# A new order for the first norm and for the last products of a hybrid RG-LRU / retention / conv-FFN block

## The chip, the cores and the metric

One core of one Trainium2 chip runs the whole program. The metric is device microseconds of one execution. Engines are named as the profile names them: PE is TensorE's matmul, PEld its weight load, DVE VectorE, ACT ScalarE, POOL GpSimd, SP SyncE.

## The reference, cut to what matters

The two ends of the computation are what the change touches: the norm of the 16 meta tokens and 512 input tokens ahead of the first projection, and the final product `w_down` with the last norm.

```python
def rms_norm(x, g):
    y = x32 * lax.rsqrt(jnp.mean(x32 * x32, axis=-1, keepdims=True) + EPS)
    return y * g
...
h = concatenate([meta_tokens, x])                 # 16 + 512 tokens, 1024 features, f32
xn = rms_norm(h, norm_mix_g)                      # first norm
z = xn @ w_in                                     # 8 parts: RNN, its gate, q, k, v, ...
... # convolution, RG-LRU, retention, mixing with w_out, h += ...
xn = rms_norm(h, norm_ffn_g)
up = causal_dwconv(xn @ w_up)
gate, val = split(up, 2)
h = h + (gelu(gate) * val) @ w_down               # 3072 -> 1024
out = rms_norm(h, norm_final_g)[:, 16:]           # final norm, meta tokens dropped
```

## The kernel before, in words

Products are f16 on TensorE. Each f32 operand is split by `split` into a high half (ScalarE, L91) and a low half (VectorE, L92), and a product is high*high + high*low + low*high. Weights come from HBM in units of at most 1 MB; SP issues their loads one after the other, ScalarE and VectorE split them into `wt` tiles, and TensorE uses them. In most of the program the tile scheduler places the instructions of each engine; within `manual_schedule` (at the start) PE, ACT and DVE keep the order in which the code is written. Each engine executes its own list in order.

At the start SP loads, in this order: 128 tokens of x, the norm's weights spread over 128 partitions (`gmix`, 512 KB), the meta tokens (16 partitions of 1024 features), the next 128 tokens, and then weights and the other tokens by turns. For one block of tokens `norm_rows` has ScalarE square and sum (L296) and take the root (L298), VectorE invert it (L300) and multiply by it and by `gmix` (L306, two halves); `norm_transpose` has TensorE transpose the rows (L313) into PSUM and `split` write them as `xh` and `xl`, the transposed f16 pair that all projections read. The blocks go 0, meta, 1, 2, 3. `keep_warm` (L392) fills TensorE with products of zeros meanwhile. `first_half(n)` (L359) is the left half (block 0, block 1 and the meta tokens) of the projection for 128 columns: 24 matmuls of 267 columns. After the last of the three first halves TensorE transposes small vectors (`ptv`) that POOL loaded by nine DMAs into `v1` and `v2`.

At the end the product with `w_down` is made as seven products by Strassen-like sums (`PRODUCTS`), for 256 columns of each half in each of two passes (`ps_`). In the last round of the second pass the seven products end one after the other, 12 matmuls each, and behind each VectorE adds what is complete (`add`, `total`), ScalarE sums squares (`square`), VectorE multiplies by the final norm's weights (`weigh`), `three_quarters` sums three of a token's four sums of squares, `inverse` takes the root with the fourth, and `rows_out` scales the rows, left half on VectorE and right half on ScalarE, and issues a 256 KB store for each. `h2p[1]` holds tokens 256 to 511 (`tt` 2 and 3), `h2p[0]` tokens 0 to 255.

Of the kernel before, what the change touches and what calls it, by code (L numbers as in the profile page):

```python
# [8 lines left out]
F32 = mybir.dt.float32  # L9
# [41 lines left out]
def hybrid_block_kernel(ctx, tc, x, meta, norm_mix_g, w_in, conv_w, conv_b, rg_a_w, rg_a_b,  # L51
# [235 lines left out]
    gmix_t = wsp.tile([P, D], F32, name="gmix", tag="wt")  # L287
    gmix = [gmix_t[:, a * 512:(a + 1) * 512] for a in range(2)]
# [33 lines left out]
    xmeta = wsp.tile([P, D], F32, name="xmeta", tag="wt")  # L322
# [47 lines left out]

    def first_rows(i):
        xn_t[i] = pair("xn")
        if i < 0:
            norm_rows(xmeta[:NM], NM, gmix, xn_t[i])
        else:
            norm_rows(xin[i // 2][:, i % 2], P, gmix, xn_t[i])

    def first_transpose(i):
        xn = xn_t.pop(i)
        if i < 0:  # L380
            norm_transpose(NM, xh[:, :, 3:3 + NM], xl[:, :, 3:3 + NM], S_XN, xn)
        else:
            c0 = 3 + NM + P * i
            norm_transpose(P, xh[:, :, c0:c0 + P], xl[:, :, c0:c0 + P], S_XN, xn)
# [25 lines left out]
    first_transpose(1)  # L410
# [4 lines left out]
    first_transpose(2)  # L415
# [5 lines left out]
    first_transpose(3)  # L421
# [678 lines left out]
    for j in range(12):  # L1100
# [10 lines left out]
        for m in range(2):  # L1111
# [3 lines left out]
            if f == KF - 1:  # L1115
# [11 lines left out]
    PRODUCTS = (("P1", "A11", "B11"), ("P6", "F6", "T2"), ("P7", "F7", "T3"), ("P4", "A22", "T4"),  # L1127
                ("P5", "F5", "T1"), ("P2", "A12", "B21"), ("P3", "F3", "B22"))
# [22 lines left out]
    def three_quarters(tt):  # L1151
        part0 = small.tile([P, 2], F32, name="part0")
        nc.vector.reduce_sum(part0[:, 0:1], sums[:, tt, 0:3], axis=mybir.AxisListType.X)
# [3 lines left out]
    def inverse(tt, part0):  # L1157
        sd = small.tile([P, 1], F32, name="sd")
        nc.scalar.activation(sd, sums[:, tt, 3:4], AF.Sqrt, scale=inv_d, bias=part0)
# [4 lines left out]
    def rows_out(tt, rs):  # L1164
        nc.vector.tensor_scalar_mul(h2[tt][:, 0:512], h2[tt][:, 0:512], rs)
        nc.sync.dma_start(o2[tt * P:(tt + 1) * P, 0:512], h2[tt][:, 0:512])
# [127 lines left out]
```

## Time and profile before

| | |
|---|---|
| median of 3 runs | 1090.39 us (1090.39 to 1091.27) |
| profiled execution | 1090.36 us, its span in the profile 1088.6 us |
| PE, PEld busy | 1064.8 us (98%), 867.7 us (80%) |
| DVE, ACT busy | 798.8 us (73%), 540.9 us (50%) |
| mean granted TensorE clock | 0.995 |
| moved by DMA | 112.01 MB, 103 GB/s over the span |

The span is from the first to the last instruction; the time of an execution has 1.8 us more around it. Starts in a timeline count from the span's start. A row of the timeline has start, length, engine, line, operation, what it writes and reads with shapes, how many instructions are merged in it, and in brackets the idle time of the engine before it with what ended it. The busy shares are means over stages with different limits: the first 28 us and the last 12 us are read by themselves below.

### The profile page before, as it was taken

The page shows a single profiled execution, that of the slowest core. Times are in us where ns is not written, and L with a number is a line of the kernel's source. Part 1 is how long each engine was busy: PE and PEld are TensorE (multiplying, and loading weights), DVE is VectorE, ACT ScalarE, POOL GpSimd, SP SyncE. Part 2 cuts the span into 40 slices and gives each one's busy share as a digit, 9 for nine tenths or more (in the row PEclk, how much of TensorE's full clock was granted, in tenths as well). Part 3 has the DMA queues.
Part 4 walks back from the last instruction along what each step waited for, and adds up shares of the span by engine and source line. Part 5 has one row for each costly group of instructions (what it writes and reads, how often), then busy time and mean ns, then how long its engine had stood idle before and what let it go on. Part 6 is the DMA issues. An engine that isn't in the chain of part 4 may idle for free.

```text
span 1088.6 us, 21084 instructions
## 1 busy us (share of the span) xinstructions
PE 1064.8 (98%) x9171; PEld 867.7 (80%) x9171; DVE 798.8 (73%) x1169; ACT 540.9 (50%) x804; POOL 5.5 (1%) x15
## 2 busy tenths in 40 slices
PE   8999999999999999999999999999999999999995
PEld 5888888865685858888888885588888888888885
DVE  6875799998795959867654542478767767888974
ACT  6558954434454636546433432364544544444433
POOL 2000000000000000000000000000000000000000
PEclk9999999999999999999999999999999999999998
DMA  6432243431212302344333343053232323114222
GB/s 206 141 116 79 78 137 117 157 118 39 79 55 67 113 25 85 106 126 127 117 117 117 117 167 124 1 193 117 79 117 79 116 86 110 40 61 149 83 78 78
DMA packets 113364, 112.01 MB, mean 103 GB/s; under 512 B 2806, under 2 KB 104788, under 8 KB 113272
## 3 DMA queue, kind: packets, MB, share of 16 engines
q1 hardware_dynamic: 112984, 110.53, 31.3%
q8 instruction: 71, 1.16, 0.4%
q0 software_dynamic: 288, 0.14, 0.0%
q14 instruction: 21, 0.17, 0.0%
HBM read 108.56 MB, written 2.10 MB: 102 GB/s over the span
## 4 chain that ended last, share of the span: by engine, by line
PE 79%; DVE 13%; ACT 5%; issue 1%; DMA 1%; ACTq 0%; SPq 0%; DVEq 0%
PE ps L346 34%; PE pm L346 13%; PE P L1139 9%; PE pa L717 6%; PE ps L777 4%; PE ps L1017 3%; DVE wt L92 3%; PE pe L717 3%; PE ps L359 2%; PE pb L717 1%; ACT wt L91 1%; DVE rnn L521 1%; PE ps L799 1%; DVE rt L818 1%; PE ptr L313 1%
## 5 line engine op out<-in xcount | busy, mean ns | idle before, releaser
L346 PEld LDWEIGHTS <-wt 128*128 128x128 f16 x4992 | 485.2, 97 | 74.8 <-DVE t L613 1.4
L92 DVE SCALAR_TENSOR_TENSOR wt<-raw,wt 128x1024 f16<-128x1024 f32 (+2 forms) x256 | 283.9, 1122 | 104.2 <-ACT wt L91 102.4
L91 ACT ACTIVATE wt<-raw 128x1024 f16<-128x1024 f32 (+2 forms) x256 | 245.1, 971 | 192.4 <-PE pm L346 58.9
L346 PE MATMUL ps<-x2h,wt 128*128 128x258 f16 x1440 | 218.8, 273 | 0.0
L346 PE MATMUL ps<-xh,wt 128*128 128x257 f16 (+2 forms) x1056 | 163.8, 275 | 1.1 <-DVE t L613 1.1
L717 PEld LDWEIGHTS <-wt 128*128 128x128 f16 x1344 | 129.6, 97 | 20.3 <-issue 1.7
L346 PE MATMUL ps<-x2l,wt 128*128 128x258 f16 x720 | 137.7, 272 | 0.0
L1096 DVE SCALAR_TENSOR_TENSOR cv<-ps,vt,cv 128x512 f32<-128x512 f32 x96 | 72.0, 750 | 54.6 <-ACT cv L1094 53.3
L346 PE MATMUL ps<-xl,wt 128*128 128x257 f16 (+2 forms) x528 | 102.2, 275 | 0.0
L1139 PE MATMUL P<-wt,act 128*128 128x256 f16 x864 | 96.3, 273 | 0.0
L1139 PEld LDWEIGHTS <-act 128*128 128x128 f16 x864 | 84.5, 98 | 9.8
L346 PE MATMUL pm<-ob,wt 128*128 128x257 f16 x768 | 87.1, 274 | 0.0
L777 PE MATMUL ps<-wt,xh 128*128 128x512 f16 x256 | 76.4, 379 | 2.3 <-DVE v L92 1.7
L717 PE MATMUL pa<-xs,wt 128*128 128x257 f16 x576 | 71.6, 273 | 0.3 <-ACT kept L722 0.3
L1094 ACT ACTIVATE cv<-ps,vt,vt 128x512 f32<-128x512 f32 x48 | 37.1, 774 | 57.6 <-PE ps L346 53.0
L346 PE MATMUL pm<-oa,wt 128*128 128x257 f16 x480 | 54.9, 274 | 0.0
L777 PEld LDWEIGHTS <-xh 128*128 128x128 f16 x256 | 24.9, 98 | 31.0 <-issue 3.0
L777 PE MATMUL ps<-wt,xl 128*128 128x512 f16 x128 | 48.3, 379 | 0.0
L1017 PE MATMUL ps<-wt,mx 128*128 128x512 f16 x192 | 44.5, 379 | 0.8 <-DVE g L905 0.8
L799 PE MATMUL ps<-sc,v 128*128 128x257 f16 (+4 forms) x384 | 31.9, 236 | 1.4 <-ACT ssum L805 1.4
L1017 PEld LDWEIGHTS <-mx 128*128 128x128 f16 x192 | 17.6, 98 | 19.2 <-issue 1.0
L359 PEld LDWEIGHTS <-wt 128*128 128x128 f16 x288 | 27.8, 97 | 6.3 <-issue 1.1
(218 smaller groups left out, 1187.3 us busy)
## 6 DMA issues: line engine op xcount, KB each, us to landing
raw<-in_w_in SPq DMA_DIRECT2D x41, 1024.0 KB, 4.8
raw<-in_w_up SPq DMA_DIRECT2D x24, 1024.0 KB, 5.0
raw<-in_w_down SPq DMA_DIRECT2D x48, 256.0 KB, 3.5
raw<-in_w_branch_ret SPq DMA_DIRECT2D x8, 1024.0 KB, 5.7
raw<-in_w_branch_rnn SPq DMA_DIRECT2D x8, 640.0 KB, 4.5
raw<-in_w_out SPq DMA_DIRECT2D x4, 1024.0 KB, 4.9
xin<-in_x SPq DMA_DIRECT2D x4, 512.0 KB, 7.3
h<-in_x SPq DMA_DIRECT2D x4, 512.0 KB, 5.1
```

Source lines behind the costliest of these rows:

```text
L91: nc.scalar.activation(hi, src, AF.Copy, scale=s)
L92: nc.vector.scalar_tensor_tensor(lo, src, s, hi, op0=ALU.mult, op1=ALU.subtract)
L313: nc.tensor.transpose(pv[:, k, :rows], xn[a][:rows, k * P:(k + 1) * P], ident[:rows, :rows])
L346: nc.tensor.matmul(ps[:, hf, :n], w(aw, k, col, P), src(ax, k, c0, n), start=k == 0 and (aw, ax) == (0, 0), stop=k == nk - 1 and aw == 1)
L359: nc.tensor.matmul(ps[:, hf, :n], w(aw, k, col, P), src(ax, k, c0, n), start=k == 0 and (aw, ax) == (0, 0), stop=k == KD - 1 and aw == 1)
L717: nc.tensor.matmul(ps[:, :257], w(wf, aw, k), src(xf_, ax, k), start=first and k == 0 and (aw, ax) == (0, 0), stop=k == 3 and aw == 1, ski ...
L777: nc.tensor.matmul(pb, xf(ax, k, XF + j0, nb), w(aw, k % 4, 0, 512), start=i == 0, stop=i == 23)
L799: nc.tensor.matmul(ps[:, hf, s0 - lo_i:257], vt[b][:, va, d * P:(d + 1) * P], st[SCP[b][0]][:, sa, o:o + hi_i - s0], start=i == 0, stop=i ...
L1017: nc.tensor.matmul(ps[:, n], mx[k][:, a, c0:c0 + P], wo[k // 2](aw, k % 2, n * 512, 512), start=j == 0, stop=j == 23)
L1094: nc.scalar.activation(vv_, ps[:, :, 2:258], AF.Identity, scale=vt2[:, 96 + ch:97 + ch], bias=b_ff[:, ch:ch + 1])
L1096: nc.vector.scalar_tensor_tensor(vv_, ps[:, :, j:j + 256], vt2[:, 48 * j + ch:48 * j + ch + 1], vv_, op0=ALU.mult, op1=ALU.add)
L1139: nc.tensor.matmul(pd[:, 256 * tt:256 * tt + 256], t[:, ax, c0 + tt * P:c0 + tt * P + P], w(wf, aw, i), start=q % 6 == 0 and tt == 0 and i ...
```

## The change

At the start the spread norm weights are no longer loaded: one row of 4 KB is loaded, TensorE spreads it with two f32 products by a row of ones (1 to 128 partitions, 512 columns each) and ScalarE copies them into `gmix`. Block 0 is first multiplied by `gmix` whole and then scaled by its factor. The meta tokens are loaded folded, a token on 8 partitions of 128 features; a product with `same` (block diagonal of ones) sums their squares over these 8 partitions, a product with `pick` lays the weights out in the same way, and one transpose serves all of them. The order of blocks is 0, 1, meta, 2, 3, and the warm-up products are 8 + 4 + 3 instead of 12 + 4 + 6. POOL builds `same` and `pick`; with `xmeta` they are taken from the pool of eight buffers that `v1` and `v2` come from too.

At the end the seven products come in another order, P5 is copied out by ScalarE, tokens 256 to 511 are completed by P4 and tokens 0 to 255 by P3, the right halves of tokens 256 to 511 are scaled by VectorE, and the early root `sq_t` reads a sum of the first pass instead of a constant.

```diff
-    gmix = [gmix_t[:, a * 512:(a + 1) * 512] for a in range(2)]
+    gmix = whole("gmix")
+    grow = whole("grow")
+    xmeta = work.tile([P, T], F32, name="xmeta", tag="w")
+    same = ...   # memset 1, two affine_selects on GpSimd: 8x8 blocks of ones
+    pick = ...   # memset 0, one affine_select: [8, 128], 1 where partition = column mod 8
...
     load(xin[0][:, 0], x2[0:P])
-    load(gmix_t, norm_mix_g.partition_broadcast(P))
-    load(xmeta[:NM], meta)
+    load(grow[0:1], norm_mix_g[None, :])
     load(xin[0][:, 1], x2[P:2 * P])
+    load(xmeta[:, 0:P], meta.rearrange("t (c f) -> (t c) f", f=P))
+    load(xmeta[0:8, P:2 * P], norm_mix_g.rearrange("(c f) -> c f", f=P))
...
-    keep_warm(12)
-    first_rows(0)
-    first_rows(-1)
-    first_transpose(0)
+    keep_warm(8)
+    for a in range(2):
+        pg = bank("pg")
+        nc.tensor.matmul(pg, ones[0:1], grow[0:1, a * 512:(a + 1) * 512], start=True, stop=True)
+        nc.scalar.activation(gmix[:, a * 512:(a + 1) * 512], pg, AF.Copy)
+    xg = whole("xg")
+    nc.vector.tensor_mul(xg, token_rows(0), gmix)
+    rs0 = rms_scale(token_rows(0), P, "n")
+    nc.vector.tensor_scalar_mul(xg[:, 0:512], xg[:, 0:512], rs0)
+    nc.vector.tensor_scalar_mul(xg[:, 512:1024], xg[:, 512:1024], rs0)
     keep_warm(4)
-    first_rows(1)
-    first_transpose(-1)
-    keep_warm(6)
+    rs1 = rms_scale(token_rows(1), P, "n")
+    nc.tensor.matmul(pmeta[:, 0, 0:P], pick[0:8, 0:P], gm, start=True, stop=True)
+    finish0 = first_transpose(0, ptr_banks())
+    nc.scalar.activation(xmeta[:, 2 * P:3 * P], xm, AF.Square, accum_out=ssm[:, 0:1])
+    nc.tensor.matmul(pmeta[:, 1, 0:1], same[:, 0:P], ssm[:, 0:1], start=True, stop=True)
+    nc.scalar.activation(ssm[:, 1:2], pmeta[:, 1, 0:1], AF.Sqrt, scale=1.0 / D, bias=eps_t)
+    for a in range(2):
+        nc.vector.scalar_tensor_tensor(xn_t[1][a], token_rows(1)[:, sl], rs1, gmix[:, sl], op0=ALU.mult, op1=ALU.mult)
+    nc.vector.reciprocal(ssm[:, 2:3], ssm[:, 1:2])
+    nc.vector.scalar_tensor_tensor(xm, xm, ssm[:, 2:3], pmeta[:, 0, 0:P], op0=ALU.mult, op1=ALU.mult)
+    keep_warm(3)
+    finish0()
+    finish1 = first_transpose(1, [pt1[:, 0], pt1[:, 1]])
+    nc.tensor.transpose(pmeta[:, 1, P:2 * P], xm, ident)
...
     for i in range(2):
         first_step()
-    first_transpose(1)
+    split(xh[:, :, 3:3 + NM], xl[:, :, 3:3 + NM], pmeta[:, 1, P:2 * P].rearrange("p (t c) -> p c t", c=8), S_XN)
+    finish1()
     first_rows(2)
     first_half(0)
...
-    PRODUCTS = (("P1", "A11", "B11"), ("P6", "F6", "T2"), ("P7", "F7", "T3"), ("P4", "A22", "T4"),
-                ("P5", "F5", "T1"), ("P2", "A12", "B21"), ("P3", "F3", "B22"))
+    PRODUCTS = (("P1", "A11", "B11"), ("P6", "F6", "T2"), ("P5", "F5", "T1"), ("P7", "F7", "T3"),
+                ("P2", "A12", "B21"), ("P4", "A22", "T4"), ("P3", "F3", "B22"))
...
-                    nc.scalar.activation(sq_t, eps_t, AF.Sqrt)
+                    nc.scalar.activation(sq_t, sums[:, 3, 0:1], AF.Sqrt)
```

In the last round the steps behind each product are now: P1: e1, add(0, left); P6: s2, add(0, right); P5: s4 (a copy by ScalarE), add(0, right); P7: s3, add(1, left), s7 = s4 + s3, add(1, right), squares, weigh(1, right); P2: add(0, left), squares, weigh(0, left), `three_quarters` of all four blocks; P4: add(1, left), squares, roots, weigh(1, left), `rows_out` of blocks 2 and 3 (both halves by VectorE); P3: for each of blocks 0 and 1 the sum, square, weigh, root and `rows_out`.

Where this moves instructions, three places show it. First ScalarE (ACT) at the very start, before the change; `xin_100` is the tile with blocks 0 and 1, `ss` a sum of squares, `sd` its root, `xh<-ptr` the high half of transposed rows:

```order
L296 ACTIVATE junk,ss<-xin_100 128x1024 [waits DMAHW0_49]
L298 ACTIVATE sd<-ss,eps_t 128x1 [waits Activation_49]
L296 ACTIVATE junk,ss<-xmeta 16x1024 [waits DMAHW2_49]
L298 ACTIVATE sd<-ss,eps_t 16x1 [waits Activation_49]
L91 ACTIVATE xh<-ptr 128x4x128 [waits PE_49] x2
L296 ACTIVATE junk,ss<-xin_100 128x1024 [waits DMAHW3_49]
L298 ACTIVATE sd<-ss,eps_t 128x1 [waits Activation_49]
L91 ACTIVATE xh<-ptr 128x4x16 [waits PE_49] x2
L91 ACTIVATE wt<-raw 128x512 [waits DMAHW4_49]
L91 ACTIVATE wt<-raw 128x512
L91 ACTIVATE xh<-ptr 128x4x128 [waits PE_49] x2
```

And after it, where `xin_111` has blocks 0 and 1, `pg` the spread weights in PSUM, `pmeta` the products of the meta tokens:

```order
L425 ACTIVATE gmix<-pg 128x512 [waits PE_49] x2
L310 ACTIVATE junk,ss<-xin_111 128x1024 [waits DMAHW0_49]
L312 ACTIVATE sd<-ss,eps_t 128x1 [waits Activation_49]
L310 ACTIVATE junk,ss<-xin_111 128x1024 [waits DMAHW2_49]
L312 ACTIVATE sd<-ss,eps_t 128x1 [waits Activation_49]
L439 ACTIVATE xmeta,ssm<-xmeta 128x128 [waits DMAHW3_49]
L441 ACTIVATE ssm<-pmeta,eps_t 128x1 [waits PE_49]
L91 ACTIVATE xh<-ptr 128x4x128 x2
```

The two copies of `gmix` now stand ahead of the squares of blocks 0 and 1, the square of block 1 ahead of the first `xh`, and the meta tokens behind both.

Second, what follows there. After the change `pt_194` holds the transposed block 1, `xin_112` blocks 2 and 3:

```order
L91 ACTIVATE wt<-raw 128x512 [waits DMAHW5_49]
L91 ACTIVATE wt<-raw 128x512
L91 ACTIVATE xh<-pmeta 128x8x16 [waits PE_49]
L91 ACTIVATE xh<-pt_194 128x4x128
L91 ACTIVATE xh<-pt_194 128x4x128 [waits DVE_49]
L310 ACTIVATE junk,ss<-xin_112 128x1024 [waits DMAHW6_49]
L312 ACTIVATE sd<-ss,eps_t 128x1 [waits Activation_49]
L91 ACTIVATE wt<-raw 128x512 [waits DMAHW7_49]
```

Before, the last four rows of the first list stood there, and these behind them:

```order
L296 ACTIVATE junk,ss<-xin_101 128x1024 [waits DMAHW5_49]
L298 ACTIVATE sd<-ss,eps_t 128x1 [waits Activation_49]
L91 ACTIVATE wt<-raw 128x512 [waits DMAHW6_49]
L91 ACTIVATE wt<-raw 128x512
L91 ACTIVATE xh<-ptr 128x4x128 [waits PE_49] x2
```

The second `xh` of block 1 now waits for VectorE (for the low half of the first one, by the count it waits for), and the square of block 2 stands behind it.

Third, VectorE (DVE) at the very end, before: `h_7669` is tokens 256 to 511, `h_7668` tokens 0 to 255, `sd` a root, `rs` its inverse, `part` three quarters of a sum of squares:

```order
L1177 SCALAR_TENSOR_TENSOR h_7668<-P_11872,h_7668 128x256 [waits DVE_49,PE_49]
L1177 SCALAR_TENSOR_TENSOR h_7668<-P_11872,h_7668 128x256
L1161 RECIPROCAL rs<-sd 128x1 [waits Activation_49] x2
L1165 TENSOR_SCALAR h_7669<-h_7669,rs 128x512 [waits DVE_49] x2
L1153 TENSOR_REDUCE part_12517<-sums 128x1 [waits Activation_49]
L1153 TENSOR_REDUCE part_12520<-sums 128x1 [waits Activation_49]
L1149 TENSOR_TENSOR h_7668<-h_7668,gfin 128x2x256
L1154 TENSOR_SCALAR part_12517<-part_12517 128x1 [waits DVE_49]
L1154 TENSOR_SCALAR part_12520<-part_12520 128x1 [waits DVE_49]
L1149 TENSOR_TENSOR h_7668<-h_7668,gfin 128x256 [waits Activation_49] x2
L1161 RECIPROCAL rs<-sd 128x1 [waits Activation_49] x2
L1165 TENSOR_SCALAR h_7668<-h_7668,rs 128x512 [waits DVE_49] x2
```

And after, where `h_7664` is tokens 256 to 511, `h_7663` tokens 0 to 255:

```order
L1199 TENSOR_TENSOR h_7664<-h_7664,gfin 128x2x256 [waits Activation_49]
L1209 TENSOR_SCALAR part_12483<-part_12483 128x1 [waits DVE_49]
L1209 TENSOR_SCALAR part_12487<-part_12487 128x1 [waits DVE_49]
L1199 TENSOR_TENSOR h_7663<-h_7663,gfin 128x256 [waits Activation_49]
L1235 SCALAR_TENSOR_TENSOR h_7663<-P_11869,h_7663 128x256
L1216 RECIPROCAL rs<-sd 128x1 [waits Activation_49] x3
L1225 TENSOR_SCALAR h_7664<-h_7664,rs 128x512 [waits DVE_49]
L1225 TENSOR_SCALAR h_7664<-h_7664,rs 128x512
L1225 TENSOR_SCALAR h_7664<-h_7664,rs 128x512 [waits DVE_49]
L1225 TENSOR_SCALAR h_7664<-h_7664,rs 128x512
L1225 TENSOR_SCALAR h_7663<-h_7663,rs 128x512 [waits DVE_49]
L1199 TENSOR_TENSOR h_7663<-h_7663,gfin 128x256 [waits Activation_49]
```

The inverses and scalings of tokens 256 to 511 (L1165 before, four L1225 after) now stand behind both parts of the sum with P3 (`h<-P`), behind the weighing of both token halves, and are four on this engine.

On ScalarE the end stood so before (`junk,sums` is a square with its sum, `part` as above):

```order
L1145 ACTIVATE junk,sums<-h_7669 128x256
L1159 ACT_TABLE_LOAD [waits DVE_49]
L1159 ACTIVATE sd<-sums,part_12474 128x1 [waits Activation_49]
L1159 ACTIVATE sd<-sums,part_12479 128x1 [waits DVE_49,Activation_49]
L1145 ACTIVATE junk,sums<-h_7668 128x256 [waits DVE_49]
L1145 ACTIVATE junk,sums<-h_7668 128x256
L1167 ACTIVATE h_7669<-h_7669,rs 128x512 [waits DVE_49] x2
L1145 ACTIVATE junk,sums<-h_7668 128x256 x2
L1159 ACTIVATE sd<-sums,part_12517 128x1 [waits DVE_49,Activation_49]
L1159 ACTIVATE sd<-sums,part_12520 128x1 [waits DVE_49,Activation_49]
L1167 ACTIVATE h_7668<-h_7668,rs 128x512 [waits DVE_49] x2
```

And after it:

```order
L1195 ACTIVATE junk,sums<-h_7664 128x256 [waits DVE_49]
L1195 ACTIVATE junk,sums<-h_7664 128x256
L1195 ACTIVATE junk,sums<-h_7663 128x256 [waits DVE_49,Activation_49]
L1214 ACTIVATE sd<-sums,part_12483 128x1 [waits DVE_49,Activation_49]
L1214 ACTIVATE sd<-sums,part_12487 128x1 [waits DVE_49,Activation_49]
L1214 ACTIVATE sd<-sums,part_12477 128x1 [waits Activation_49]
L1195 ACTIVATE junk,sums<-h_7663 128x256 [waits DVE_49]
L1223 ACTIVATE h_7663<-h_7663,rs 128x512 [waits DVE_49]
L1214 ACTIVATE sd<-sums,part_12480 128x1 [waits Activation_49]
L1223 ACTIVATE h_7663<-h_7663,rs 128x512 [waits DVE_49]
```

The table load is gone from this stretch (it stands behind the squares of the first pass), and the first root now follows seven squares.

More of the change, by code (lines that the diff above doesn't have):

```diff
@@ L285, in hybrid_block_kernel, with whole @@
     nc.vector.memset(xl[:, :, 0:3], 0.0)
-    gmix_t = wsp.tile([P, D], F32, name="gmix", tag="wt")
-    gmix = [gmix_t[:, a * 512:(a + 1) * 512] for a in range(2)]
+    def whole(name):
+        return wsp.tile([P, D], F32, name=name, tag="wt")
+    gmix = whole("gmix")
+    grow = whole("grow")
+    xmeta = work.tile([P, T], F32, name="xmeta", tag="w")
+    same = work.tile([P, T], F32, name="same", tag="w")
+    nc.gpsimd.memset(same[:, 0:P], 1.0)
+    for base, mult, step in ((0, 1, -8), (7, -1, 8)):
+        nc.gpsimd.affine_select(out=same[:, 0:P], in_=same[:, 0:P], compare_op=ALU.is_ge, fill=0.0, base=base,
+                                pattern=[[step, NM], [0, 8]], channel_multiplier=mult)
+    pick = work.tile([P, T], F32, name="pick", tag="w")
+    nc.gpsimd.memset(pick[0:8, 0:P], 0.0)
+    nc.gpsimd.affine_select(out=pick[0:8, 0:P], in_=pick[0:8, 0:P], compare_op=ALU.not_equal, fill=1.0, base=0,
+                            pattern=[[0, NM], [-1, 8]], channel_multiplier=1)
     def pair(name):
@@ L369, in first_half, with token_rows, first_transpose, finish @@
         project_half(ps, wviews[u], col, xf, HR, 0)
+    def token_rows(i):
+        return xin[i // 2][:, i % 2]
     def first_rows(i):
         xn_t[i] = pair("xn")
[L373 to L378, printed above, removed]
-        xn = xn_t.pop(i)
[L380 to L384, printed above, removed]
+        norm_rows(token_rows(i), P, [gmix[:, 0:512], gmix[:, 512:1024]], xn_t[i])
+    def first_transpose(i, banks):
+        xn = xn_t.pop(i)
+        c0 = 3 + NM + P * i
+        pvs = []
+        for a in range(2):
+            pv = banks[a].rearrange("p (b c) -> p b c", c=P)
+            for k in range(4):
+                nc.tensor.transpose(pv[:, k], xn[a][:, k * P:(k + 1) * P], ident)
+            pvs.append(pv)
+        def finish():
+            for a in range(2):
+                sl = slice(4 * a, 4 * a + 4)
+                split(xh[:, sl, c0:c0 + P], xl[:, sl, c0:c0 + P], pvs[a], S_XN)
+        return finish
     warm = work.tile([P, 512], F16, name="warm", tag="w")
@@ L1162, in inverse, with rows_out @@
         return rs
-    def rows_out(tt, rs):
-        nc.vector.tensor_scalar_mul(h2[tt][:, 0:512], h2[tt][:, 0:512], rs)
-        nc.sync.dma_start(o2[tt * P:(tt + 1) * P, 0:512], h2[tt][:, 0:512])
-        nc.scalar.activation(h2[tt][:, 512:1024], h2[tt][:, 512:1024], AF.Copy, scale=rs)
-        nc.sync.dma_start(o2[tt * P:(tt + 1) * P, 512:1024], h2[tt][:, 512:1024])
+    def rows_out(tt, rs, two):
+        for n in range(2):
+            sl = slice(n * 512, (n + 1) * 512)
+            if two and n == 1:
+                nc.scalar.activation(h2[tt][:, sl], h2[tt][:, sl], AF.Copy, scale=rs)
+            else:
+                nc.vector.tensor_scalar_mul(h2[tt][:, sl], h2[tt][:, sl], rs)
+            nc.sync.dma_start(o2[tt * P:(tt + 1) * P, sl], h2[tt][:, sl])
     for ps_ in range(2):
@@ L1202, in hybrid_block_kernel @@
                 if ps_ == 1:
-                    nc.scalar.activation(sq_t, eps_t, AF.Sqrt)
+                    nc.scalar.activation(sq_t, sums[:, 3, 0:1], AF.Sqrt)
+                add(0, left, e1, un)
             elif nm == "P6":
                 s2 = total(pv, e1, "s2")
-                add(0, left, e1, un)
+                add(0, right, s2, -un)
+            elif nm == "P5":
+                s4 = work.tile([P, 512], F32, name="s4", tag="w")
+                nc.scalar.activation(s4, pv, AF.Copy)
+                add(0, right, s4, -un)
             elif nm == "P7":
@@ L1209, in hybrid_block_kernel @@
                 add(1, left, s3, un)
[L1210 to L1217 removed]
+                s7 = total(s4, s3, "s7")
                 add(1, right, s7, -un)
```

60 lines of the change are left out of this document (34 added, 26 removed).

## Prediction, made blind

> **What bounds the kernel now.** I read the page first, then the chain that ended last, and its two ends in the timeline.
>
> ```profile
> span 1088.6 us, 21084 instructions
> ...
> PE 79%; DVE 13%; ACT 5%; issue 1%; DMA 1%; ACTq 0%; SPq 0%; DVEq 0%
> ```
>
> The chain itself, in order of time (start, length, what):
>
> ```profile
> 1.18 5.66 DMA gmix<-in_norm_mix_g
> ...
> 14.68 0.70 DVE xl L92
> ...
> 15.43 2.80 PE ps L359 x23
> 18.23 0.45 PE ptr L313 x4
> ...
> 25.20 0.61 DVE wt L92
> ...
> 27.56 8.37 PE ps L359 x72
> ...
> 1039.97 29.49 PE P L1139 x270
> ...
> 1074.99 0.68 DVE s L1182
> 1075.67 0.60 DVE h L1149
> ...
> 1077.83 1.28 ACT L1159
> ```
>
> TensorE is the bound from 27.56 to the end of its products; the change does not touch that stretch, where the rows keep their order. What it does touch are the two ends: up to 27.56 ScalarE and VectorE set the pace, and after TensorE has stopped (about 1077.3) they do so again until the stores leave. So the sum is a start term and an end term; a shift of either passes whole into the time.
>
> **The start, as it is.**
>
> ```profile
> 1.43 4.57 PE L392 MATMUL ps<-warm 128*128 128x512 f16 x12 [1.43 <-DVE warm L387]
> 4.68 1.06 ACT L296 ACTIVATE junk<-xin 128x1024 f16<-128x1024 f32 x1 [2.22 <-DMA xin<-in_x]
> 5.87 0.30 ACT L298 ACTIVATE sd<-ss,eps_t 128x1 f32<-128x1 f32 x1
> 6.19 0.17 DVE L300 RECIPROCAL rs<-sd 128x1 f32<-128x1 f32 x1 [4.82 <-ACT sd L298]
> 6.98 1.42 DVE L306 SCALAR_TENSOR_TENSOR xn<-xin,rs,gmix 128x512 f32<-128x512 f32 x2 [0.62 <-DMA gmix<-in_norm_mix_g]
> 7.70 0.51 POOL L438 DMA_DIRECT2D v<-in_norm_ffn_g  x1 [1.99 <-DMA v<-in_rnn_conv_w]
> 8.96 1.40 DVE L306 SCALAR_TENSOR_TENSOR xn<-xmeta,rs,gmix 16x512 f32<-16x512 f32 x2
> 10.29 1.27 DVE L92 SCALAR_TENSOR_TENSOR xl<-ptr,xh 128x512 f16<-128x512 f32 x2
> 13.35 1.29 DVE L92 SCALAR_TENSOR_TENSOR wt<-raw,wt 128x512 f16<-128x512 f32 x2
> 15.02 1.06 ACT L296 ACTIVATE junk<-xin 128x1024 f16<-128x1024 f32 x1
> 16.73 1.42 DVE L306 SCALAR_TENSOR_TENSOR xn<-xin,rs,gmix 128x512 f32<-128x512 f32 x2
> 18.06 1.04 PE L313 MATMUL ptr<-ident,xn 128*128 128x128 f32 x8
> 27.01 0.27 PE L440 MATMUL ptv<-ident,v 128*128 128x128 f32 x1
> ```
>
> The spread norm weights (512 KB) hold VectorE for 0.62 us at 6.98; by then the squares are long done.
>
> **The start, as it becomes.** The 512 KB go; a 4 KB row is queued in their place, right behind the first token tile, which was there at 4.68. Eight warm-up products instead of twelve end near 5.0 (first eight of the row at 1.43, 0.43 us each), so the row costs TensorE nothing or up to 0.5 us. The two spreading products are f32, 512 columns. The nearest rows are the f32 products of the head norm in the timeline, and for the copy out of PSUM that of the end in the groups (their time, mean ns of one):
>
> ```profile
> 300.13 1.14 PE L814 MATMUL ps<-ssum,ones 128*128 128x257 f32 x4 [0.37 <-DVE ssum L807]
> 301.11 0.49 PE L717 MATMUL pe<-xs,wt 128*128 128x257 f16 x3
> ```
>
> ```profile
> L1201 ACT ACTIVATE e<-P 128x512 f32<-128x512 f32 x1 | 0.6, 598 | 12.5 <-PE P L1139 12.5
> ```
>
> Two products of 257 columns (four records) take 0.98 us to the next matmul, so 1024 columns take 1.75 (without the first weight load) to 1.95, and twice that if the clock is still at half. I take 1.85. Gmix's second half is copied out at C = 5.0 + 1.85 + 0.15 (1.14 less 0.98, a product's way out) + 0.6 = 7.6, against 6.84 for the DMA (1.18 + 5.66).
>
> From C on I walk down the new rows. ScalarE has put both copies ahead of the squares that it did at 4.68: square and root take 1.5 (4.68 to 6.17), the reciprocal 0.2, so the first tile's factor comes at C + 1.7 and its rows (two scalings, 0.86) at C + 2.6. The second tile's root follows 1.4 later: factor C + 3.1, rows (1.42) C + 4.5. Then VectorE does, in this order: reciprocal and rows of the folded meta tile (0.45, an estimate for 128 columns), xl of tile 0 (1.27), the weights' low halves (1.29), meta's xl (0.2, likewise), first half of tile 1's xl (0.7): C + 8.4 less an overlap of about 0.1 = C + 8.3 = 15.9, where TensorE's second matmul now starts at 15.43. What leaves VectorE (1.40 for the meta rows, 1.42 for tile 0) is about what comes (1.2 for the product with gmix, twice the 0.60 at 1075.67; 0.86, 0.45), and C is 0.8 later. ScalarE's second xh of tile 1 waits for that xl (the order shows the wait), so the square of tile 2 starts at 16.2 and not at 15.02, tile 2's rows end 3.1 later at 19.3 and not at 18.15, and its second four transposes start at 19.35 instead of 18.5: **+0.85**. Everything to 27.56 hangs on these and shifts with them.
>
> That is with TensorE at full clock. But look at its clock, window by window (length, PE busy, granted clock):
>
> ```profile
> 5.15:8.56 3.41, 1.54 (x9) 1.00 1.00 315
> 8.56:11.97 3.41, 3.41 (x16) 0.50 1.10 377
> 11.97:15.38 3.41, 2.75 (x18) 1.00 0.42 165
> ```
>
> A window in which TensorE was busy 45% was followed by one at half clock, although in that one it had no pause; 81% busy was followed by full clock. In the new order TensorE has, from 11.97 to 15.38, three warm-up products at most, nine transposes and then nothing until 15.9: some 0.8 to 1.0 us, 24 to 30%. If the windows fall as here, 15.38 to 18.80 is at half clock. Then the 24 matmuls of the first half product (2.80 us at full clock) do 13 by 18.8 (0.22 each) and the other 11 by 20.0 (0.11 each), and the transposes start at 20.0 instead of 18.06: **+1.95**. I take this one, since the row that it is nearest to (45%) is on the far side of it. With the windows placed otherwise it reaches +2.7 (all 24 at 0.22, 5.3 us).
>
> [...]
>
> Costed at nothing: five more small POOL operations and the pick and same products (done before 8, while VectorE waits for factors); one more SP issue (0.4 us, ahead of weights that are split only at 13.35, and behind 508 KB less); the shuffle of PSUM tiles. POOL's nine loads of small vectors now wait for a buffer that the pick product frees, at about 8 and not at 1.44; the last one then is issued near 14.5 and lands by 20, 8 us before its transposes (27.01 plus the shift). Without that cover each us late would be a us.
>
> **The end**, first in the timeline, then one group and two windows (the last number is GB/s):
>
> ```profile
> 1079.12 0.48 ACT L1159 ACTIVATE sd<-sums,part 128x1 f32<-128x1 f32 x2
> 1079.72 0.86 DVE L1165 TENSOR_SCALAR h<-h,rs 128x512 f32<-128x512 f32 x2
> 1080.21 0.36 SPq L1166 DMA_DIRECT2D out<-h  x1
> 1080.31 1.32 ACT L1167 ACTIVATE h<-h,rs 128x512 f32<-128x512 f32 x2
> ...
> 1083.51 0.33 SPq L1166 DMA_DIRECT2D out<-h  x1
> ...
> 1084.90 0.41 SPq L1168 DMA_DIRECT2D out<-h  x1
> ```
>
> ```profile
> L1145 ACT ACTIVATE junk<-h 128x256 f32<-128x256 f32 x8 | 3.2, 404 | 5.9 <-DVE h L1177 5.9
> ```
>
> ```profile
> 1084.30:1087.10 2.80, 0.00 (x0) 0.00 (x0) 0.00 (x0) 0.03 (x1) 0.00 (x0) 0.50 1.00 373
> 1087.10:1088.60 1.50, 0.00 (x0) 0.00 (x0) 0.00 (x0) 0.00 (x0) 0.00 (x0) 0.50 0.01 3
> ```
>
> Now the stores leave in two lots of four: tokens 256 to 511 from 1080.21, the others from 1083.51. The second lot (1.05 MB) fills the DMA engines for 2.8 us, and 1.5 us after its last byte the span ends.
>
> Removed: the 1.28 us table load in the chain at 1077.83 (the root that should load it early now reads a sum of the first pass, so it stays there). Moved: P4 becomes the sixth product of seven, so tokens 256 to 511 get their last sum one product later, and the second half of their rows is scaled on VectorE (two more scalings, 0.8) instead of ScalarE (1.32); P5 is copied out by ScalarE (0.6). I walked the rows of VectorE and ScalarE with 0.60 to 0.61 for a 512-wide operation (as at 1075.67) (0.70 behind its own input), 0.42 a square, 0.24 a root, 0.41 a scaling, 0.07 a small one. The same walk over the rows before puts the first store at 1080.1 and the last at 1084.9. In the new order: P4's sum ends at 1077.35; seven squares keep ScalarE until 1079.8; VectorE goes through three weighings (0.6 each), one late sum, and ten small operations, and has the constants of tokens 256 to 511 only at 1080.6; roots; the late half sum of P3; reciprocals at 1081.2; first scaled half at 1081.9, where its store starts: 1.7 later than now. The others follow every 0.45 us; the last starts at 1085.05 (now 1084.90). The table load's 1.28 is thus spent by in-order work ahead of the first root. And then all eight stores (2.1 MB) come in one lot: at 373 to 390 GB/s that is 5.4 to 5.6 us from 1082.8 (0.9 after the first issue, as 1083.51 to 1084.4), so to 1088.2 instead of 1087.1: **+1.1**. Were the DMA engines no limit, the last issue alone would give +0.15; if the stores are also a little later, +1.5.
>
> **Sum.** The profiled execution took 1090.36 us (span 1088.6 and 1.8 around it), the median shown is 1090.39: 1090.36 + 1.95 + 1.1 = 1093.4.
>
> **Rivals.**
> 1. The clock holds. The start is +0.85: 1092.3, no slower than the 0.2% (2.2 us) which a measurement of this kernel can just tell from no change. [...] Chance 0.24.
> 2. The table load's time is kept. If the first store starts before 1080.8, the DMA engines are done by 1087.1 again, and the end term is -0.4 to +0.2; with the start, 1091.0 to 1092.5. Against it: sixteen VectorE rows stand between P4's sum and the first scaling. Chance 0.12.
> 3. The spreading comes late or cold: the row lands after 5.5, or the products run at half clock (3.5 us), C is 1 to 1.9 later: 1094.2 to 1095.2. Chance 0.08.
> 4. Faster. The 512 KB less let the first tiles' weights and rows land 1.4 us earlier, and VectorE, not C, sets the start: -1; with rival 2's end it would be 1088.0. Against it: after 6.98 none of ScalarE's and VectorE's rows above ends a wait for a DMA. Chance 0.06.
>
> **How the numbers follow.** The forecast itself has 0.50. The range 1091.0 to 1095.0 goes from rival 2's low end to just short of rival 3's high end. Slower by over 0.2% (over 1092.6): 0.50 + 0.08 + a third of rival 1 = 0.66; within: 0.28; faster: 0.06.
>
> **What would show it.** Right: gmix ready near 7.6; the second matmul of the first half product near 15.9, with 0.22 us spacing and a granted clock of 0.5 up to about 18.8; no table load after 1070; the first store 1.7 us later against the last product than now, all stores in one lot of 5.4 us. Wrong: full clock from 15.4 on, or stores in two lots again.

## The result, and the profile after

The changed kernel takes 1093.29 us in the median of 7 runs (1092.97 to 1094.91), before 1090.62 (1090.20 to 1091.45): a ratio of 1.0028, 95% interval 1.0017 to 1.0040. The forecast was 1093.4. Its seven executions form two groups, four at 1092.97 to 1093.29 and three at 1094.87 to 1094.91; the profiled one is the fastest (1092.97, span 1091.2, 2.6 more than before).

The chain that ended last, at the start (start, length, what):

```profile
1.50 3.48 PE ps L414 x8
4.98 1.92 PE pg L424 x4
6.92 0.60 ACT gmix L425
...
9.75 1.94 PE ptr L399 x8
11.69 0.22 PE pmeta L440 x2
11.90 1.30 PE ps L414 x3
13.21 1.71 PE pt L399 x8
14.91 0.21 PE pmeta L452
...
15.95 0.70 DVE xl L92
16.68 0.60 ACT xh L91
...
29.47 8.37 PE ps L373 x72
```

The long run of first products starts at 29.47 instead of 27.56, **+1.91**. From 9.75 to 15.1 the chain runs through TensorE: the transposes of block 0 and of block 1 take 1.94 and 1.71 us, and three warm-up products 1.30. TensorE's clock in windows of 3.41 us, placed where the records change (length, PE busy with its count, granted clock, DMA share, GB/s); the recorded changes of this trace are at 4.73, 8.14, 14.97 and 1083.34, those of the kernel before at 5.15, 8.56, 11.97 and 1080.34, 1, 2 or 313 times 3.413 us apart:

```profile
1.32:4.73 3.41, 3.23 (x8) 1.00 0.74 265
4.73:8.14 3.41, 3.41 (x11) 1.00 0.99 327
8.14:11.55 3.41, 1.93 (x11) 0.50 1.01 353
11.55:14.97 3.42, 3.42 (x15) 0.50 0.15 41
14.97:18.38 3.41, 2.10 (x17) 1.00 0.60 182
```

The clock is at half from 8.14 to 14.97, although TensorE had no pause in the window before that; and it is full in the window for which half was forecast. In the first row 1.00 cannot be right: eight warm-ups took 3.48 us, 0.43 each, and three of them took 1.30 at 11.90, in a window recorded at 0.50. The clock record of this trace begins with the rise at 4.73, that of the kernel before with one at 5.15, and the profile shows 1.00 for all that lies ahead.

The end, in the timeline and one window (the last number is GB/s):

```profile
1071.15 8.02 PE L1189 MATMUL P<-wt,act 128*128 128x256 f16 x72
1083.17 2.05 DVE L1225 TENSOR_SCALAR h<-h,rs 128x512 f32<-128x512 f32 x5
1083.66 4.18 SPq L1226 DMA_DIRECT2D out<-h  x8
1084.50:1089.70 5.20, 0.00 (x0) 0.00 (x0) 1.61 (x5) 0.72 (x1) 0.00 (x0) 0.50 1.04 397
```

TensorE stops at 1079.17 (1077.31 before), the first store is issued 4.5 us later (2.9 before), all eight leave in one lot at 397 GB/s, and the span ends 12.0 us after TensorE instead of 11.3: **+0.75**. Together the terms are 2.66; the two profiled executions differ by 2.61 us. Nothing of it comes from the stretch between (1049.7 us from the first long product to TensorE's end in both).

### The profile page after: what moved, and what is told of

The parts are those of the page before. It is cut to its first block, busy times and chain, and to the rows that moved or that the text cites. A ratio compares the mean times of both kernels' runs of the same rounds, so it can differ in the third digit from the quotient of the medians.

```text
span 1091.2 us, 21083 instructions
## 1 busy us (share of the span) xinstructions
PE 1066.2 (98%) x9165; PEld 868.8 (80%) x9165; DVE 799.4 (73%) x1172; ACT 540.9 (50%) x805; POOL 6.8 (1%) x20
## 4 chain that ended last, share of the span: by engine, by line
PE 76%; DVE 14%; ACT 7%; issue 1%; DMA 1%; ACTq 0%
PE ps L360 32%; PE pm L360 12%; PE P L1189 10%; PE pa L767 6%; PE ps L827 4%; PE ps L1067 3%; DVE wt L92 3%; PE pe L767 2%; PE ps L373 2%; ACT wt L91 2%; PE pb L767 1%; DVE rnn L571 1%; PE ps L849 1%; DMA raw<-in_w_up 1%; ACT L623 1%
```

## Experiments

**The start alone.** The changed kernel up to `PRODUCTS`, the kernel before from there on.

> The changed start with the end of before. Theory 'two separate terms': the start alone costs what the trace of the changed kernel shows there, 29.47 - 27.56 = +1.9 us, so about 1092.5 against 1090.6, with the last product and the first store as far apart as before (2.9 us). Rival 'one disturbs the other' (the later start moves the phase of the clock or of the weight loads, and the end pays for it): less than +1.0 or more than +2.7.

Measured: 1092.39 (1091.30 to 1093.99, 11 runs), ratio 1.0016 (1.0007 to 1.0025): eight executions up to 1092.47, three at 1093.98 to 1093.99. The profiled one is of the upper three; TensorE's rows of its timeline, and the chain's last:

```profile
1.50 3.60 PE L414 MATMUL ps<-warm 128*128 128x512 f16 x8 [1.50 <-DVE warm L409]
5.03 3.78 PE L424 MATMUL pg<-grow,ones 1*128 1x512 f32 x4
8.74 1.89 PE L414 MATMUL ps<-warm 128*128 128x512 f16 x4
...
11.67 1.94 PE L399 MATMUL ptr<-ident,xg 128*128 128x128 f32 x8 [0.32 <-DVE xg L429]
...
31.40 0.68 PE ps L373 x5
```

The spreading takes 3.78 us instead of 1.98, and the long run starts at 31.40, another 1.9 later. That is the second group, and the prediction's third rival. The first store is issued 2.9 us after TensorE stops (1083.96 and 1081.06), as before. The terms add up (this run and the next one together 1.0021, within the interval of the whole), so the first theory holds, with a start term of 1.9 or 3.8.

In this trace TensorE is slow from its start: eight warm-ups in 3.60 us (3.48 in the changed kernel's execution above), the spreading in 3.78 (1.98), the next four warm-ups in 1.89 (1.04), the eight transposes of block 0 in 1.94 and of block 1 in 1.91; a matmul of the first half product at 17.91 takes 0.28, as at full speed. The profile shows 1.00 all this time. From 1.50 to 10.6 TensorE had no pause, 3.8 us of it with products that read a single row, and stayed at half speed. In the execution above, one window ended at 4.73 with 3.23 us of the warm-ups in it, and the clock rose. For an execution of the slower group such a point can be had as an estimate: in the run with the right halves on ScalarE below, whose spreading takes 3.78 us too, the clock falls behind TensorE's end at about 1085.85 (0.67 granted from 1085.57 to 1086.40), and 317 steps of 3.413 us back from there is 3.82, where 2.3 us of the warm-ups had run. On that estimate it would be the phase of the windows, that is, where they fall against the start of the program, that parts the groups; no run shows it directly.

**The end alone.** The kernel before up to `PRODUCTS`, the changed one from there on.

> The start of before with the changed end. Theory 'two separate terms': TensorE stops at 1077.3 as before, the first store is issued 4.5 us later instead of 2.9, the span ends 12.0 us after TensorE instead of 11.3: +0.75, about 1091.35. Rival 'the end costs nothing by itself' (what the trace of the changed kernel shows there comes with the start): within 0.2 of before.

Measured: 1091.51 (1090.85 to 1092.84, 11 runs), ratio 1.0005 (0.9996 to 1.0014). The time alone does not part the two; the trace does. The last products and the stores:

```profile
1069.17 8.02 PE L1139 MATMUL P<-wt,act 128*128 128x256 f16 x72
1081.67 4.19 SPq L1176 DMA_DIRECT2D out<-h  x8
```

TensorE stops at 1077.19, the stores begin 4.48 us later, the span ends at 1089.3, 12.1 after TensorE: the end costs its 0.75 by itself. ScalarE's roots wait 0.95 us there for VectorE's sums, so the time of the table load that has gone is not gained.

The medians of the spans are a second measure: 1090.7 with the start alone and 1089.3 with the end alone against 1088.85 before, +1.85 and +0.45. They differ from the times because 1.7 to 3.2 us lie around the span in the kernels with the old start, and 1.7 to 2.0 in those with the new one; why, no run shows. The spans of the kernel before themselves lie between 1088.1 and 1090.6.

The start of this trace also bears on the prediction's view of the clock. Counted back from the clock's fall at about 1079.84 (0.96 granted from 1078 to 1080) in 315 steps of 3.413 us, an estimate, a window lies from 4.63 to 8.04. In it TensorE was busy for 1.52 us, as little as in the window of before that was followed by half clock (1.54, from 5.15 to 8.56), and here TensorE stayed at full speed, as a row of the timeline shows (the same four products took 1.91 us before):

```profile
8.71 1.03 PE L392 MATMUL ps<-warm 128*128 128x512 f16 x4
```

So in these two traces the busy share alone does not say what the clock does.

**The early table load alone, on the kernel before.**

```
-                    nc.scalar.activation(sq_t, eps_t, AF.Sqrt)
+                    nc.scalar.activation(sq_t, sums[:, 3, 0:1], AF.Sqrt)
```

> Before with one edit: the early root reads a sum of the first pass, so the table is loaded there and not at 1077.83. Theory 'the load was on the path and the freed time is only lost by the new order': the roots come 1.28 us earlier, all stores move with them, -1.2 us, about 1089.4. Rival 'the time is taken by the next wait' (VectorE's sums, or the DMA engines, take over): -0.4 to 0.

Measured: 1090.88 (1089.69 to 1093.10, 11 runs), ratio 1.0002 (0.9993 to 1.0011). Neither theory as written. The end of its timeline:

```profile
1073.80 4.20 PE L1139 MATMUL P<-wt,act 128*128 128x256 f16 x37
1079.58 0.87 DVE L1165 TENSOR_SCALAR h<-h,rs 128x512 f32<-128x512 f32 x2
1080.08 0.36 SPq L1166 DMA_DIRECT2D out<-h  x1
1081.22 0.74 DVE L1177 SCALAR_TENSOR_TENSOR h<-P,h 128x256 f32<-128x256 f32 x2
1085.05 0.41 SPq L1168 DMA_DIRECT2D out<-h  x1
```

Counted from TensorE's end (1078.00) the first store leaves at 2.1 instead of 2.9: 0.8 earlier, where the theory had 1.28, since VectorE's weighing (1078.99) now stands between the inverses and the scalings. And the scheduler now puts the sum with P3 (1081.22) behind the scalings (1079.58), where before it stood ahead of them, and the second lot's last issue gains only 0.55 (7.05 after TensorE, 7.6 before). The span ends 10.7 after TensorE, 0.6 sooner; in this execution the start was 0.8 later (28.35), and the median shows no gain that its interval can tell.

**Both high halves of block 1 first** (the wait of ScalarE for VectorE taken away).

```
             for a in range(2):
-                split(xh[...], xl[...], pvs[a], S_XN)
+                nc.scalar.activation(xh[...], pvs[a], AF.Copy, scale=S_XN)
+            for a in range(2):
+                nc.vector.scalar_tensor_tensor(xl[...], pvs[a], S_XN, xh[...], ...)
```

> The changed kernel with one edit: for block 1 both high halves are written ahead of both low halves in the code, and ScalarE's second one no longer waits for VectorE's first low half. Theory 'that wait holds back block 2': the square of block 2 starts about 0.6 us earlier (16.6 instead of 17.27), and the long run of first products 0.6 to 0.7 earlier (28.8 instead of 29.47): 1092.6 against 1093.3 in runs of the same kind. Rival 'the slow transposes set it all' (TensorE at half clock from 8.1 to 15.0): no gain beyond 0.2, since VectorE's low halves come no earlier.

Measured: 1094.45, six runs (1092.97, two at 1094.2, three at 1094.69), ratio 1.0032 (1.0021 to 1.0044): no gain. The profiled execution belongs with the one of the first experiment (spreading 3.78); two rows of its timeline and the last of the chain:

```profile
17.26 1.08 ACT L405 ACTIVATE xh<-pt 128x512 f16<-128x512 f32 x2
18.37 1.29 DVE L408 SCALAR_TENSOR_TENSOR xl<-pt,xh 128x512 f16<-128x512 f32 x2 [0.68 <-ACT xh L405]
31.25 0.79 PE ps L373 x6
```

The wait went to the other side: now VectorE's first low half waits for both high halves, and the first half product starts 0.5 later (19.12, 18.63 there). The square of block 2 does start 0.9 earlier (18.21, 19.10 there), but its transposes then stand behind that product, and the long run starts only 0.15 earlier. The edit is in the function that serves all four blocks, so the other blocks' high halves move too.

**Without the three warm-ups.**

```
-    keep_warm(3)
```

> The changed kernel without the three warm-up products between the transposes of block 0 and block 1. Theory 'they stand on the path' (1.30 us at half clock, in the chain at 11.90): block 1's transposes start at 11.9 instead of 13.2, VectorE's low halves take over as the limit, the long run of first products starts 0.3 to 0.6 earlier (29.0 instead of 29.47, or 30.9 instead of 31.4 where the spreading ran at half clock): about -0.4. Rival 'they bring the clock up': without them the window is less busy, the clock rises 3.4 us later, the first half product runs at half clock, +1 to +2.7.

Measured: 1096.17 (1094.49 to 1096.54, five runs), ratio 1.0042 (1.0029 to 1.0054): the rival. Two rows of the chain that ended last (its spreading took 3.78 too):

```profile
18.01 5.30 PE ps L373 x23
...
33.05 1.02 PE ps L373 x8
```

TensorE reaches the product 0.6 earlier (18.01, 18.63 in the first experiment) and then does it at half speed, 5.30 us instead of 2.80; the long run starts 1.65 later (33.05, 31.40 there). Nothing ahead of the product was at full speed: eight warm-ups took 3.59 us, the spreading 3.78, the transposes 1.94 and 1.95, and the four transposes behind it still took 0.87 (0.45 before). So the product is slow because TensorE had not yet come to full speed, not because it fell from it. Group by group it is about 1.4 us more than the changed kernel (1094.5 and 1096.2 against 1093.1 and 1094.9).

**The norm weights by DMA.** The edit of the next experiment, but without its last line.

> The changed kernel with the norm weights loaded spread (512 KB) as before; no row, no spreading products, no copies; 8 + 4 warm-ups then follow each other. Theory 'the spreading is the cost' (late, and its one-row products leave TensorE cold): gmix is there at 6.9 instead of 7.5 or 9.4, no executions with a start 1.9 us later, start 28.6 to 29.0, about 1092.3 in the median. Rival 'the order of the rows is the cost': the start stays at 29.3 to 29.6, as in the faster executions of the changed kernel (1093.1).

Measured: 1095.73 (1095.59 to 1096.37, five runs), ratio 1.0043 (1.0031 to 1.0056). It tells nothing of the spreading, for the zeros of the warm-ups landed elsewhere, as two rows of the chain show:

```profile
7.78 0.27 DVE warm L408
8.10 4.48 PE ps L413 x12
```

Without the copies on ScalarE the order put VectorE's `warm` behind its wait for `gmix`; the twelve warm-ups began at 8.10 and stood ahead of the transposes, at half speed for most of their length (4.48 us; 5.30 where no product of the twelve is at full speed, in the run of one-row warm-ups below).

**The norm weights by DMA, zeros early.**

```
-    load(grow[0:1], norm_mix_g[None, :])
+    load(gmix, norm_mix_g.partition_broadcast(P))      # spreading products and copies removed
+    nc.vector.memset(warm, 0.0)                        # moved up, behind ones
```

> The changed kernel with the norm weights loaded spread (512 KB), 8 + 4 warm-ups in a row, and the zeros for the warm-ups written at 1.2 us as in the changed kernel (in the run before this one VectorE wrote them only behind its first multiplication, at 7.78, and TensorE began at 8.1). Theory 'the spreading and the cold TensorE are the cost': gmix there at 6.5 to 6.9, block 0 transposed from 8.2, the second matmul of the first half product at 14.5 to 15.5, the long run of first products at 27.0 to 28.0, and with the changed end 1091.0 to 1092.0. Rival 'the order of the rows is the cost': the long run at 29 or later, 1093.

Measured: 1091.28 (1091.01 to 1092.17, 11 runs), ratio 0.9999 (0.9990 to 1.0008), against 1.0028 (1.0017 to 1.0040) with the spreading. No execution is near 1093, as the first theory has it. In the medians of the spans it is 1089.6 against 1089.0 before, 0.6 more, which is about what the changed end inside it costs (0.75); so the new order of blocks itself costs nothing that can be told. The profiled one is among its longer ones (1091.94), its long run at 28.50, between the two forecasts, its transposes again at half speed (1.97 us for eight, 1.04 at 18.06 before; two rows of TensorE's timeline, one of the chain):

```profile
1.44 4.13 PE L413 MATMUL ps<-warm 128*128 128x512 f16 x12 [1.44 <-DVE warm L279]
8.75 1.97 PE L400 MATMUL ptr<-ident,xg 128*128 128x128 f32 x8
28.50 5.50 PE ps L374 x47
```

**One-row warm-ups, on the kernel before.**

```
-            nc.tensor.matmul(early[0][:, 0], warm[:, 0:P], warm, ...)
+            r = 1 if n == 12 else P
+            nc.tensor.matmul(early[0][:, 0], warm[:r, 0:P], warm[:r], ...)
```

> Before with one edit: the first 12 warm-up products read one row (1 partition) instead of 128; same columns, same count, same busy time. Theory 'the clock counts rows at work, not busy time': all 12 take 0.43 us each (5.1 us in all), and the matmuls behind them, to 9 us at least, are still at half speed; time 0 to +2. Rival 'busy time counts': as before, the clock rises at about 5.1, the 12 take 4.6 us, no change.

Measured: 1091.44 (1090.62 to 1092.62, 10 runs), ratio 1.0002 (0.9993 to 1.0011); the long run at 29.44 in the profiled execution (1092.32). TensorE's timeline:

```profile
1.43 5.30 PE L393 MATMUL ps<-warm 1*128 1x512 f16 x12 [1.43 <-DVE warm L387]
7.82 1.94 PE L313 MATMUL ptr<-ident,xn 128*128 128x128 f32 x8 [1.09 <-DVE xn L306]
9.55 1.91 PE L393 MATMUL ps<-warm 128*128 128x512 f16 x4
```

All twelve took 0.43 or so, and everything behind them to 14.9 ran at half speed, as the first theory has it. TensorE came to full speed among the eight transposes that begin at 14.89 (1.44 us together, 1.94 at 7.82, 1.04 at 19.95), by their length at about 15.7, an estimate. Counted back from it in steps of 3.41 us, the window from about 2.0 to 5.5 held nothing but one-row products, without a pause, and TensorE stayed at half speed. Before, the window from 1.73 to 5.15 held nothing but the same products with 128 rows, and the clock rose at 5.15; full speed also comes among the twelve of the run above (4.13 us for all) and of the end alone (4.33). One thing stays open: the window from about 8.9 to 12.3 was full here too, with 128-row transposes, four 128-row warm-ups and 16-row transposes, and did not raise the speed (the six warm-ups at 12.36 took 2.74 us, 1.47 before), while before the one from 8.56 to 11.97, with nearly the same products, was followed by full clock. The median does not move, so this shows a difference in speed, not a price; the spans of four of the ten executions, the profiled one among them, are 1090.3 to 1090.7, of the other six 1088.7 to 1089.0.

**Spreading with 128 rows.**

```
-        nc.tensor.matmul(pg, ones[0:1], grow[0:1, ...], ...)
+        nc.tensor.matmul(pg, ones, grow[:, ...], ...)     # grow zeroed first, its row loaded behind xmeta; zeros of the warm-ups written earlier
```

> The changed kernel with its two spreading products over 128 rows (the row of weights and 127 rows of zeros, by 128 rows of ones) instead of 1 row: same columns, same time at the same clock. The row is loaded behind the zeros, about 1 us later. Theory 'one-row products leave the clock down': the products now count, TensorE is at full speed by 8.5 at the latest in every execution (transposes of block 0 in 1.0 us, not 1.94), and no execution is 1.8 us above the others; median 1092.5 to 1093.3. Rival 'the clock has nothing to do with the rows': two groups as in the changed kernel, both about 1 us later, 1094 and 1095.9.

Measured: 1093.52 (1093.03 to 1096.98, 11 runs), ratio 1.0028 (1.0019 to 1.0037): six at 1093.03 to 1093.52, four at 1094.65 to 1095.06, one at 1096.98. The theory is wrong in what it made of the time: groups remain. Two rows of TensorE's timeline:

```profile
5.90 1.95 PE L425 MATMUL pg<-grow,ones 128*128 128x512 f32 x4 [1.26 <-DMA grow<-in_norm_mix_g]
10.72 1.74 PE L402 MATMUL ptr<-ident,xg 128*128 128x128 f32 x8 [1.59 <-DVE xg L430]
```

The spreading is at full speed, but the transposes are mostly at half again (1.74 us; 1.94 in the changed kernel, 1.04 at 18.06 before): TensorE stood still for 1.59 us ahead of them. In this execution it had come to full speed among the eight warm-ups (3.21 us, 3.60 at half speed in the first experiment), ahead of the spreading, so the trace does not show what the 128 rows of the spreading do to the clock.

**Right halves of tokens 256 to 511 on ScalarE.**

```
-                        rows_out(tt, parts[tt], False)
+                        rows_out(tt, parts[tt], True)
```

> The changed kernel with the right halves of tokens 256 to 511 scaled by ScalarE again. Theory 'the stores are bound by the DMA engines': the first store leaves 4.5 us after TensorE as now, the last is issued up to 0.8 earlier, but the 2.1 MB still take 5.4 us from 0.9 after the first issue: within 0.3 of the changed kernel. Rival 'VectorE's five scalings in a row set the end': -0.6 to -0.8.

Measured: 1093.41 (1092.43 to 1094.97, 11 runs), ratio 1.0025 (1.0016 to 1.0034), two groups as in the changed kernel. VectorE has three scalings in a row instead of five, the first store again leaves 4.5 us after TensorE, and the eight issues take as long as with five (timeline):

```profile
1085.08 1.26 DVE L1225 TENSOR_SCALAR h<-h,rs 128x512 f32<-128x512 f32 x3
1085.57 4.18 SPq L1226 DMA_DIRECT2D out<-h  x8
```

The span ends 12.0 after TensorE. The expected earlier last issue did not come: the last store starts 3.6 us after the first in both. So VectorE's scalings do not set the end, but whether the DMA engines do, this run cannot tell. What speaks for them is that they are full (share 1.04) for 5.2 us at 397 GB/s in the changed kernel, and for as long in the last experiment below, whose stores begin earlier; then only an earlier first store helps.

**Early table, late sum first.** The kernel before with the early table load and this, in the last round of the second pass:

```
             elif nm == "P2": ...
+                    for tt in (2, 3): left_out(tt, parts[tt])       # left halves of rows_out
+                    weigh(1, right)                                 # from P5
+                    for tt in (2, 3): right_out(tt, parts[tt])
             else:
+                with tc.high_priority():
+                    for tt in (0, 1): ...                           # add(0, right), square, inverse
+                weigh(0, left)
+                ...                                                 # left_out, weigh(0, right), right_out
```

> Before with the early table load, and the sum with P3 placed on VectorE ahead of the scalings of tokens 256 to 511 (where the scheduler had moved it behind them in the run with the early table alone). Theory 'two lots overlap': P3's sum ends 1.5 us after TensorE, the last store is issued 6.2 us after it (7.6 before, 7.05 with the early table alone), and the span ends 10.4 to 10.7 us after TensorE instead of 11.3: about -0.7. Rival 'the DMA engines set it': the span ends no earlier than with the early table alone (10.7 after TensorE), however early the last issue.

Measured: 1090.53 (1089.22 to 1091.89, 11 runs), ratio 0.9993 (0.9984 to 1.0002). In the trace TensorE stops at 1077.2, the first store leaves at 1079.95, and the span ends 10.4 later than TensorE, 0.9 less than before; in the median the gain is just inside the noise.

**The same with 16 warm-ups.**

```
-    keep_warm(12)
+    keep_warm(16)
```

> The kernel with the early table and the late sum first, with 16 warm-up products at the start instead of 12. Theory 'the spread between executions is the clock at the start': TensorE is at full speed in more of them when the transposes begin at 7.8; the median falls by 0.3 to 0.8 towards the lowest time (1089.2). Rival 'the products come in the way': at half speed 16 take 6.9 us and end at 8.3, 0.5 after the transposes could start: +0.3 to +0.5.

Measured: 1089.43 (1089.17 to 1090.50, 11 runs), ratio 0.9985 (0.9976 to 0.9994): faster than both kernels (by 0.15% against the one before); seven of eleven lie within 1089.17 to 1089.70. TensorE at the start, and the end (the window's last number is GB/s):

```profile
1.43 5.87 PE L392 MATMUL ps<-warm 128*128 128x512 f16 x16 [1.43 <-DVE warm L387]
7.81 1.23 PE L313 MATMUL ptr<-ident,xn 128*128 128x128 f32 x8 [0.50 <-DVE xn L306]
1078.44 1.34 DVE L1179 SCALAR_TENSOR_TENSOR h<-P,h 128x512 f32<-128x512 f32 x3
1081.80:1087.00 5.20, 0.00 (x0) 0.00 (x0) 1.93 (x8) 2.10 (x5) 0.00 (x0) 0.50 1.04 399
```

The gap ahead of the transposes shrinks to 0.50, the sum with P3 directly follows that with P2, and the stores leave in one lot that begins 2.7 us after TensorE. That the narrower spread (1.3 us, 2.7 without the four products) is the clock's doing is not shown: the profiled execution is one of the four longer ones (1090.31), TensorE fell to half speed among the six warm-ups at 12.00 (1.95 us, 1.47 before; the eight transposes behind them 1.91, 1.05 before), and its long run starts at 28.48, later than before. The intervals of this and the previous kernel overlap.

## Why the prediction was right, point by point

- **The size.** +1.91 and +0.75 were measured in the profiled execution, +1.95 and +1.1 forecast. The total is right; its first term came about in another way than the one written, and that the sizes match there is luck. The forecast was 0.85 for the wait for the low half and 1.1 for a first half product at half speed. Measured is that same wait, 1.08 us later than walked (the second four transposes of block 2 start at 20.43, not 19.35), and no slow product.
- **C.** `gmix` was ready at 7.52, forecast 7.6. Right for the lower group; in the upper one it is 9.44, which is rival 3 ("late or cold", 1094.2 to 1095.2) and is what three of seven executions did (1094.9). A chance of 0.08 looks too small for that. The step that was weak: "I take 1.85", the price at full speed. Eight warm-ups of 0.43 us end at about 5.0 to 5.1, 3.5 to 3.6 us after the start, hardly longer than one window of 3.41, and on the estimate above it is a matter of where the window falls whether the clock has risen by then (with one ending at 4.73 it had; with one ending at about 3.82 it had not).
- **The walk from C to the second matmul.** Forecast 15.9, measured 16.70. The factor and rows of block 0 (10.0) and block 1 (11.9) came as walked; from there the chain goes through TensorE, which the walk had left out. Its half-speed transposes held up the sums of the meta tokens (root at 11.94), and those ScalarE's high halves. VectorE waits three times on this way, 0.34, 0.23 and 0.19 us: the missing 0.8.
- **The clock.** "If the windows fall as here, 15.38 to 18.80 is at half clock": wrong. The window there was full, with matmuls 0.11 apart; the half-speed stretch came earlier, at 8.14, and cost about as much on another part of the path. The premise was that busy time decides. But 4.73 to 8.14 was busy throughout and was followed by half clock; in the end alone a window as little busy as the one that the forecast leaned on (1.52 us, 1.54) was not; and in the start alone TensorE ran without a pause from 1.50 to 10.6 and stayed at half (the transposes at 11.67 took 1.94 us), 3.8 us of it on one-row products. A first half product at half speed exists where the three warm-ups are taken away (5.30 us for the 23 matmuls), but there TensorE had not been at full speed before. Which work raises the clock the runs show in one pair of windows: the one full of one-row products (about 2.0 to 5.5) was followed by half speed, the one full of the same products with 128 rows (1.73 to 5.15, before) by full clock.
- **Rivals.** 1 (clock holds, 1092.3) was right that 15.38 to 18.80 is at full clock, and had the wrong time, since the clock had fallen earlier (at 8.14). 2 (first store earlier) and 4 (start earlier) did not come. Two of their sums are off: 2's low end is 1090.36 + 0.85 - 0.4 = 1090.8, not 1091.0, and 4 with 2's end is 1090.36 - 1 - 0.4 = 1089.0, not 1088.0.
- **The wait for the low half** (+0.85) was real, and in the path as forecast (VectorE at 15.95, ScalarE at 16.68). Taking it away does not give its price back: it came back on VectorE, and the start gained 0.15.
- **The end.** First store 1.7 later forecast, 1.58 measured; one lot, 5.2 us at 397 GB/s where 5.4 to 5.6 was taken: that, and the 0.1 of the first store, is why +1.1 became +0.75. The last store starts 3.6 us after the first, not 3.15. "The table load's 1.28 is spent by in-order work" holds: on the old order the same edit moved the first store by 0.8, on the new one ScalarE waits for VectorE's sums.
- **Costed at nothing**: POOL's last load was issued at 12.97, its transposes ran at 28.9 without waiting for it. Right.

## What to carry to other kernels

Check TensorE's speed at the start by the length of a known product, not by the clock column (here eight warm-ups took 3.48 us and four later ones 1.04, both under 1.00), and walk the chain through TensorE at half speed until a trace shows otherwise: a transfer replaced by a small product can lose more than the transfer cost (here the ratio is 1.0028 with the spreading, 0.9999 with the transfer). Warm-up products are not padding: removing three cost about 1.4 us here. At the end of a kernel look at when the first store can leave and at what rate the stores then go: here two more scalings on VectorE behind that moment cost nothing (12.0 us from TensorE's end to the span's with five and with three; DMA share 1.04 meanwhile with five, 0.99 to 1.07 with three), and a first store 1.6 us later cost 0.75.

## What the runs showed of the hardware

- Products that read one row are at work by the busy column but did not bring TensorE to full speed in the run with one-row warm-ups: a window filled with them (about 2.0 to 5.5, an estimate) was followed by half speed, one filled with the same products of 128 rows (1.73 to 5.15 in the kernel before) by full clock. Eight transposes took 1.94 us behind the former, 1.23 in the kernel with sixteen 128-row ones.
- The profiles show a granted clock of 1.00 ahead of the first recorded change (4.73 in the changed kernel), and in the start alone throughout from 1.00 to 26.00, though there one product of 512 columns took 0.45 to 0.47 us in the first 9 us of TensorE's products, where it took 0.26 at 6.82 in the changed kernel. The mean clock of an execution of the changed kernel is accordingly higher (0.996 to 0.997) in the slower group than in the faster (0.993).
- A full-speed TensorE fell back to half after a window with 1.54 us of work in the kernel before (5.15 to 8.56), and after a full one (4.73 to 8.14) with some 1.1 us of 128-row and 2.3 us of one-row and eight-row work in the changed one; with 1.52 us, in the end alone (4.63 to 8.04, an estimate), it stayed at full. Which level of which work decides was not measured.
